# Expert loop written out in program order on three engines, router called for tiles 0-3 and 4-7 behind the next tile's norm

## The chip, the cores and the metric

One core of a Trainium2 chip runs the whole kernel. The metric is device time in microseconds (us), the median of three runs.

## What is computed

Two blocks after each other on a sequence of 1024 tokens of width 1024, in fp32. The first block has two layers, each a mixer, a layer norm, a mixture of experts and a layer norm. The change touches the mixture of experts and what stands around it. The second block (two layers of retention, latent attention and gated linear attention) is not touched.

```python
# hier_moe, cut: 1024 tokens, 4 groups of 8 experts, two experts for each token
gate = g_p * softmax(top_v)                 # of the two best experts in the best group
expert_id = g_idx[:, None] * 8 + top_i
...
def run_block(args):                        # one block of up to 128 tokens of one expert
    xb, e = args
    h = silu(xb @ w_gate[e]) * (xb @ w_up[e])
    return h @ w_down[e]                    # w_gate, w_up 1024 x 512; w_down 512 x 1024
...
out = zeros((N, D)).at[tok_pad].add(y * w_pad[:, None])
# layer: h = layer_norm(ALPHA * h + mix); h = layer_norm(ALPHA * h + hier_moe(h))
```

## The kernel before

**Products.** A product in fp32 is made of three passes with rounded operands (`mm3`, lines 85 to 87): high by high, high by low, low by high. So each operand is first cut by `split` (lines 80 and 81): ScalarE copies the rounded high part, VectorE subtracts it to get the low part. Below, "hi" is the L80 copy and "lo" the L81 subtraction. `lo_eng` can send the subtraction to GpSimd.

**One expert.** Its tokens are gathered into `xg` by an indirect DMA that GpSimd issues (L718), turned by TensorE (L95), and cut into `xgh` and `xgl`. The weights come as six pieces of 1 MB: gate and up for the first half of the inner size, gate and up for the second half, and two of down. They are called g0, u0, g1, u1, d0 and d1 below. Each piece is loaded into one of nine raw slots by SyncE's queue, and cut into one of four `wcut` buffers. The products gate and up end in `gu` (two accumulators in PSUM), then come silu (L743, ScalarE) and the product of both (L744, VectorE), the turn of the result (L754) with its cut into `hh` and `hl`, the down product into the two `accy`, and its scaling in two halves `yo` (L772 on ScalarE, L773 on VectorE). GpSimd issues the scatter of `yo` (L774). The loop runs over 32 experts. In it the down product of expert e-1 stands behind gate and up of expert e, and the gather of expert e+3 behind that; there are four `xg` buffers.

**What sets the order.** A scheduler orders the instructions of each engine. It starts from the order in which the code issues them, and moves an instruction ahead of others where its own estimate has it ready. An engine then runs its instructions strictly in the order that results. Nothing in the code of before ties the loop to an order.

**Ahead of the loop.** `proj_ln` projects the mixer's output for eight tiles of 128 tokens, adds the residual (L923) in two halves n = 0 and 1, and normalizes (lines 468 to 477). For tile t-1 it then turns the normalized rows (`turn`, L568) and multiplies them with the router's weights (`logits`, L578), between the products of tile t; tile 7 has its own call at the end. `logits` adds the bias on VectorE (L579) and calls `route` at the end of tiles 3, 5 and 7, for the tiles (0,4), (4,6) and (6,8). `route` is a chain of some 35 small VectorE instructions. In it M (L633) lets TensorE make the positions `pos` (L636), those make the match matrix A (L691), and TensorE sums A with the codes in `Bm` to the slot table `tb` and the gates `tg` (L704). After the last call the table becomes the index `idx` (L708), on which the first gather waits.

Expert 0's four weight pieces are cut while `proj_ln` still runs, and their lo parts go to GpSimd (the argument `None if e else nc.gpsimd`).

Of the kernel before, what the change touches and what calls it, by code (L numbers as in the profile page):

```python
# [19 lines left out]
S = 1024  # L20
# [49 lines left out]
class Ctx:  # L70
# [18 lines left out]
    def transpose_split(self, src, hi, lo, ps):  # L89

        nc = self.nc
        for g in range(2):
            tp = ps.tile([P, 4, P], F32, tag="tp", name=self.name("tp"))
            for k in range(4):
                nc.tensor.transpose(tp[:, k], src[4 * g + k], self.ident)  # L95
            self.split(tp, hi[:, 4 * g:4 * g + 4], lo[:, 4 * g:4 * g + 4])
# [366 lines left out]
def layer_norm(g, pool, z, dst, gb, eps=1e-5):  # L463
# [11 lines left out]
    for c in range(2):  # L475
        sl = slice(c * 512, c * 512 + 512)
        nc.vector.scalar_tensor_tensor(dst[:, sl], z[:, sl], rs, gb[:, 1, sl], op0=ALU.mult, op1=ALU.add)
# [34 lines left out]
class Moe:  # L512
# [12 lines left out]
    def __init__(self, g, layer, wp, pool, h, hd, yd):  # L525
# [11 lines left out]
        self.views, self.raws = [], []  # L537
# [35 lines left out]
    def logits(self, t, hT, ps):  # L573
# [31 lines left out]
    def route(self, t0, t1, pool, ps):  # L605
# [38 lines left out]
        if t1 == NT:  # L644
            self.slots()
# [35 lines left out]
    def windows(self, pool, t0, t1):  # L681
# [9 lines left out]
        B.tensor_tensor(A, g.iota[:, None, None, :].broadcast_to(shape), self.pos[:, :, ts, None].broadcast_to(shape), op=ALU.is_equal)  # L691
# [14 lines left out]
    def slots(self):  # L706

        self.g.nc.vector.tensor_scalar(self.idx, self.tb, 2.0 * S, None, op0=ALU.add)  # L708
# [11 lines left out]

    def x_t(self, xg, pool, ps):
        g = self.g
        xh = pool.tile([P, KD, P], F32R, tag="xgh", name=g.name("xgh"))
        xl = pool.tile([P, KD, P], F32R, tag="xgl", name=g.name("xgl"))
        g.transpose_split(pair_blocks(xg), xh, xl, ps)
        return xh, xl

    def gate_up(self, wg, wu, x, pool, ps, lo_eng=None, between=None):
        g, nc = self.g, self.g.nc
        acc = [ps.tile([P, 512], F32, tag=f"acc{j}", name=g.name("gu")) for j in range(2)]  # L730
        for kb in range(2):
            if kb == 1 and between is not None:
                between()
            for j, w in enumerate((wg, wu)):
                if w is None:
                    wh, wl = self.next_w(lo_eng)
                else:
                    wh, wl = self.one_w(self.rows(w, kb))
                for k in range(4):
                    kk = 4 * kb + k  # L740
                    g.mm3(acc[j], x[0][:, kk], x[1][:, kk], wh[:, k], wl[:, k], kk == 0, kk == KD - 1)
# [16 lines left out]
    def down(self, wd, mid, xg, gate, yidx, pool, ps, no_dep):  # L758

        g, nc = self.g, self.g.nc  # L760
        hh, hl = mid
        y = pool.tile([P, D], F32, tag="yo", name=g.name("yo"))
        cols = [slice(n * 512, n * 512 + 512) for n in range(2)]
        accs = [ps.tile([P, 512], F32, tag="accy", name=g.name("accy"), bufs=2) for _ in cols]
        for kb in range(2):
            wh, wl = self.next_w() if wd is None else self.one_w(self.down_rows(wd, kb))
            for acc, sl in zip(accs, cols):
                for j in range(2):
                    k = 2 * kb + j
                    g.mm3(acc, hh[:, k], hl[:, k], wh[:, j, sl], wl[:, j, sl], k == 0, k == 3)  # L770
        for acc, sl in zip(accs, cols):
# [9 lines left out]
    def run(self, xgs, ahead):  # L781
# [4 lines left out]
        with tc.tile_pool(name=g.name("moe"), bufs=2, **near) as pool, tc.tile_pool(name=g.name("moeps"), bufs=2, space=PSUM, **near) as ps:  # L786
# [4 lines left out]
            down = lambda e, mid: self.down(None, mid, buf(e), self.sg[:, :, e:e + 1], self.idx[:, 1, e:e + 1], pool, ps, no_dep)  # L791
# [1265 lines left out]
```

## Time and profile before

| | |
|---|---|
| median of 3 runs | 3633.43 us (3632.14 to 3643.11) |
| the profiled execution | 3632.52 us, of which span 3630.7 us |
| mean granted clock of TensorE | 0.952 |
| TensorE busy | 3325.3 us (92%) |
| VectorE busy | 2443.4 us (67%) |
| ScalarE busy | 1818.7 us (50%) |
| GpSimd busy | 821.1 us (23%) |

The span runs from the first to the last instruction on the chip; the profiled execution takes 1.8 us more than that. In the rows below PE is TensorE, PEld its weight load, DVE VectorE, ACT ScalarE, POOL GpSimd and SP SyncE. A busy share is an average over stages that have different limits. The mixtures of experts lie at 721 to 1316 us (first layer) and 1637 to 2232 us (second layer).

### The profile page before, as it was taken

How to read it: one execution, taken by the hardware profiler on the slowest of the kernel's cores; microseconds unless marked ns; L12 is line 12 of the kernel's file. 1: busy time of each engine (PE TensorE's matmuls, PEld its weight loads, DVE VectorE, ACT ScalarE, POOL GpSimd, SP SyncE). 2: the span in 40 equal slices, each digit the busy share in tenths (PEclk: the TensorE clock that was granted, in tenths of full speed). 3: DMA queues.
4: the chain of work that ended last, by engine and by line, in shares of the span. 5: the costliest groups of instructions: out<-in, count | busy, mean ns of one | idle time of the engine just before them, and what ended most of it. 6: DMA issues, size and time to landing. Idle time of an engine off the chain costs nothing.

```text
span 3630.7 us, 44256 instructions
## 1 busy us (share of the span) xinstructions
PE 3325.3 (92%) x16820; PEld 2733.2 (75%) x16820; DVE 2443.4 (67%) x2912; ACT 1818.7 (50%) x2509; POOL 821.1 (23%) x591
## 2 busy tenths in 40 slices
PE   8889899799999969979999995799989899998988
PEld 7777787688887758768888774686777688776876
DVE  5564887699999976568999998634256435324753
ACT  3113673288877743317887774222457411234761
POOL 0000441333321123032332222424002113300120
PEclk9999999799999989989999997899999999998999
DMA  6554623499999960248999996211222542122245
GB/s 224 183 205 145 160 70 138 159 345 387 377 354 359 346 242 24 95 141 316 382 388 362 358 350 248 79 38 24 84 94 83 179 130 40 29 69 97 75 125 161
DMA packets 289358, 695.79 MB, mean 192 GB/s; under 512 B 43898, under 2 KB 140956, under 8 KB 272692
## 3 DMA queue, kind: packets, MB, share of 16 engines
q1 hardware_dynamic: 268404, 650.91, 51.7%
q0 software_dynamic: 18432, 33.60, 2.5%
q10 hardware_dynamic: 2304, 8.39, 0.6%
q8 instruction: 135, 2.21, 0.2%
q14 instruction: 83, 0.68, 0.1%
HBM read 625.59 MB, written 98.66 MB: 199 GB/s over the span
## 4 chain that ended last, share of the span: by engine, by line
PE 46%; DVE 7%; ACT 3%; issue 3%; POOL 3%; DMA 2%; SPq 0%; POOLq 0%; ACTq 0%; DVEq 0%
PE A L87 4%; PE A L85 4%; PE A L86 4%; PE acc L87 3%; PE acc L85 3%; PE acc L86 3%; PE gu L86 3%; PE gu L87 2%; PE gu L85 2%; DVE wcut L81 2%; PE accy L85 1%; PE accy L87 1%; PE accy L86 1%; PE T L1717 1%; PE o L1738 1%
## 5 line engine op out<-in xcount | busy, mean ns | idle before, releaser
L81 DVE TENSOR_TENSOR wcut<-wraw,wcut 128x2048 fp32r<-128x2048 f32 (+1 forms) x393 | 879.7, 2266 | 74.0 <-ACT wcut L80 70.9
L80 ACT ACTIVATE wcut<-wraw 128x2048 fp32r<-128x2048 f32 (+1 forms) x401 | 752.8, 1898 | 90.9 <-PE gu L87 47.1
L86 PE MATMUL gu<-wcut,xgh 128*128 128x512 f32 x1024 | 412.6, 403 | 14.0 <-DVE wcut L81 13.9
L85 PE MATMUL gu<-wcut,xgh 128*128 128x512 f32 x1024 | 404.7, 399 | 0.0
L87 PE MATMUL gu<-wcut,xgl 128*128 128x512 f32 x1024 | 402.8, 393 | 0.0
L774 POOL DMA_INDIRECT yd<-yo,idx x64 | 187.2, 2925 | 857.5 <-DVE yo L773 836.2
L85 PE MATMUL A<-h,whi 128*128 128x512 f32 (+1 forms) x736 | 286.6, 390 | 6.2 <-ACT h L80 3.3
L87 PE MATMUL A<-h,wlo 128*128 128x512 f32 (+1 forms) x736 | 281.3, 382 | 3.8 <-DVE wlo L81 3.8
L86 PE MATMUL A<-h,whi 128*128 128x512 f32 (+1 forms) x736 | 282.2, 384 | 0.9 <-DVE h L81 0.9
L86 PEld LDWEIGHTS gu<-wcut,xgh 128*128 128x128 f32 x1024 | 193.8, 189 | 74.6 <-DVE wcut L81 37.6
L80 ACT ACTIVATE whi<-wraw 128x1024 fp32r<-128x1024 f32 (+2 forms) x86 | 71.1, 856 | 333.8 <-PE A L86 249.8
L87 PEld LDWEIGHTS gu<-wcut,xgl 128*128 128x128 f32 x1024 | 193.1, 189 | 38.1 <-DVE xgl L81 0.5
L85 PEld LDWEIGHTS gu<-wcut,xgh 128*128 128x128 f32 x1024 | 192.0, 189 | 39.1 <-ACT xgh L80 0.5
L86 PE MATMUL accy<-wcut,hh 128*128 128x512 f32 x512 | 203.1, 397 | 0.0
L81 DVE TENSOR_TENSOR wlo<-wraw,whi 128x1024 fp32r<-128x1024 f32 (+2 forms) x86 | 82.5, 975 | 178.1 <-ACT whi L80 177.8
L87 PE MATMUL accy<-wcut,hl 128*128 128x512 f32 x512 | 200.6, 392 | 1.1 <-DVE hl L81 1.1
L85 PE MATMUL accy<-wcut,hh 128*128 128x512 f32 x512 | 191.7, 393 | 0.0
L85 PEld LDWEIGHTS A<-h,whi 128*128 128x128 f32 x736 | 144.4, 197 | 34.3 <-ACT h L80 4.5
L87 PEld LDWEIGHTS A<-h,wlo 128*128 128x128 f32 x736 | 143.7, 195 | 31.4 <-DVE wlo L81 4.7
L86 PEld LDWEIGHTS A<-h,whi 128*128 128x128 f32 x736 | 144.3, 196 | 27.3 <-issue 3.1
L718 POOL DMA_INDIRECT xg<-hd,idx x64 | 136.4, 2131 | 44.9 <-DVE idx L708 24.1
L772 ACT ACTIVATE yo<-accy,sg 128x512 f32<-128x512 f32 x128 | 87.2, 681 | 105.2 <-PE accy L87 105.2
(509 smaller groups left out, 7847.9 us busy)
## 6 DMA issues: line engine op xcount, KB each, us to landing
wraw<-in_moe_w_gate SPq DMA_DIRECT2D x128, 1024.0 KB
wraw<-in_moe_w_up SPq DMA_DIRECT2D x128, 1024.0 KB
wraw<-in_moe_w_down SPq DMA_DIRECT2D x128, 1024.0 KB
spare<-in_ada_w SPq DMA_DIRECT2D x48, 512.0 KB
wraw<-in_w_in SPq DMA_DIRECT2D x40, 512.0 KB
y<-yd SPq DMA_DIRECT2D x16, 1024.0 KB
wraw<-in_attn_w_qkv SPq DMA_DIRECT2D x12, 1024.0 KB
mx<-mixd SPq DMA_DIRECT2D x24, 512.0 KB
```

Of the source, the lines that this page charges most:

```text
L80: self.nc.scalar.activation(hi, src, AF.Copy)
L81: (lo_eng or self.nc.vector).tensor_tensor(lo, src, hi.bitcast(F32), op=ALU.subtract)
L85: mm(out, wh, xh, start=start, stop=False)
L86: mm(out, wh, xl, start=False, stop=False)
L87: mm(out, wl, xh, start=False, stop=stop)
L718: self.g.nc.gpsimd.indirect_dma_start(out=xg, out_offset=None, in_=self.hd, in_offset=bass.IndirectOffsetOnAxis(ap=idx, axis=0), bounds_ch ...
L772: nc.scalar.activation(y[:, sl], acc, AF.Copy, scale=gate[:, 0])
L774: st = nc.gpsimd.indirect_dma_start(out=self.yd, out_offset=bass.IndirectOffsetOnAxis(ap=yidx, axis=0), in_=y, in_offset=None, bounds_chec ...
L1717: nc.tensor.transpose(tp[:, j - j0], p[:, j * P:j * P + P], g.ident)
L1738: nc.tensor.matmul(o, vv[j // 4][:, j % 4, h], pT[:, j], start=j == 0, stop=j == i)
```

## The change

**The loop.** It is written out over 34 steps. Step e issues the result of expert e-2, the gather of expert e+2, gate and up of expert e, the turn of the middle of expert e-1, the turns of the tokens of expert e+1, and the down product of expert e-1. The cuts stand between them, three pieces ahead of TensorE. `in_order` chains every instruction of TensorE, ScalarE and VectorE in the loop to the one that was issued before it on the same engine, so that the scheduler leaves them in program order; it adds no wait. GpSimd and the DMA queues are not chained. The first four gathers are issued ahead of the loop (before: three).

**The router.** `logits` returns its accumulator, and the bias and `route` become `routed`, which is called behind the layer norm of the next tile with `issue_after(normed)`: the scheduler may issue them only after the last instruction of that norm. `route` is called for the tiles (0,4) and (4,8).

**Expert 0's cuts.** All lo parts are now on VectorE. The third piece is issued behind A of the last `route` (`matched`) and the fourth behind `idx` (`slots`).

```diff
+    @contextmanager
+    def in_order(self, *engines):
+        traced = self.nc.cur_bb.bb.instructions
+        n, last = len(traced), {}
+        yield
+        for i in reversed(traced[:n]):
+            last.setdefault(i.engine, i)
+        for i in traced[n:]:
+            if i.engine in engines:
+                if i.engine in last:
+                    self.tc.add_manual_dep(i, last[i.engine].name, mybir.DependencyInfo(mybir.DependencyClass.NoSync, ...
+                last[i.engine] = i
...
-    def next_w(self, lo_eng=None):
-        if not self.raws:
+    def cut(self):
+        if not self.raws and self.views:
             self.prefetch(1)
-        return self.wp.split(self.raws.pop(0), lo_eng)
+        if self.raws:
+            after = self.after.pop(0) if self.after else None
+            with ExitStack() if after is None else self.g.tc.issue_after(after):
+                self.cuts.append(self.wp.split(self.raws.pop(0)))
...
-        nc.vector.tensor_add(self.lg[:, t], lp[:, :36], self.br)
-        for t0, t1 in ((0, 4), (4, 6), (6, 8)):
+        return t, lp
+
+    def routed(self, t, lp, ps):
+        self.g.nc.vector.tensor_add(self.lg[:, t], lp[:, :36], self.br)
+        for t0, t1 in ((0, 4), (4, 8)):
             if t + 1 == t1:
                 self.route(t0, t1, self.rt, ps)
...
         if t1 == NT:
-            self.slots()
+            matched = self.matched.ins
+            self.after = [None, None, matched, self.slots()]
...
-            for e in range(3):
+            for e in range(4):
                 gather(e)
-            nxt = self.x_t(buf(0), pool, ps)
-            for e in range(32):
...
-                nsg = self.gate_up(None, None, x, pool, ps, None if e else nc.gpsimd, between)
-                if e > 0:
-                    down(e - 1, mid[0])
-                if e + 3 < 32:
-                    gather(e + 3)
-                sg = nsg
-            down(31, self.turn_mid(sg, pool, ps))
+            x = self.x_t(buf(0), pool, ps)
+            for _ in range(3):
+                self.cut()
+            with g.in_order(mybir.EngineType.PE, mybir.EngineType.Activation, mybir.EngineType.DVE):
+                for e in range(34):
+                    self.cut()
+                    if e > 1:
+                        result(e - 2, acc)
+                        if e + 2 < 32:
+                            gather(e + 2)
...
+                    if gu:
+                        self.gu(gu[0], x, self.cuts.pop(0), 0)
+                        self.cut()
+                        self.gu(gu[1], x, self.cuts.pop(0), 0)
+                    if 0 < e < 33:
+                        mid = self.turn_mid(sg, pool, ps)
+                    if e + 1 < 32:
+                        nxt = self.x_new(pool)
+                        self.x_half(buf(e + 1), nxt, 0, ps)
+                    if gu:
+                        self.cut()
+                        self.gu(gu[0], x, self.cuts.pop(0), 1)
+                        if e + 1 < 32:
+                            self.x_half(buf(e + 1), nxt, 1, ps)
...
+                        nc.scalar.activation(sg, gu[0], AF.Silu)
+                        self.cut()
+                        self.gu(gu[1], x, self.cuts.pop(0), 1)
+                        nc.vector.tensor_mul(sg, sg, gu[1])
+                        x = nxt
+                    if 0 < e < 33:
...
+                        for kb in range(2):
+                            if gu:
+                                self.cut()
+                            self.dn(acc, mid, self.cuts.pop(0), kb)
...
-                        moe.logits(t - 1, hT, ps)
+                        done = moe.logits(t - 1, hT, ps)
                 zn = z[:, n * 512:n * 512 + 512]
                 nc.vector.scalar_tensor_tensor(zn, zn, ALPHA, acc[n], op0=ALU.mult, op1=ALU.add)
-            layer_norm(g, pool, z, z, gb)
+            normed = layer_norm(g, pool, z, z, gb)
+            if done is not None:
+                with tc.issue_after(normed):
+                    moe.routed(*done, ps)
...
-        moe.logits(NT - 1, moe.turn(NT - 1, ps, pool), ps)
+        moe.routed(*moe.logits(NT - 1, moe.turn(NT - 1, ps, pool), ps), ps)
```

What stands in a row is shown at three places. The line numbers of the changed kernel are others: `route`'s M is L659 there, A is L719, `idx` L736, the residual L980, the norm 485 to 494, the router's bias L605, silu L855, `yo` L804 and L805.

VectorE, first layer, around the residual of tile 7 (`h_5427`, half n = 1 on `acc_6402`), before; the rows ahead of the residual are the end of the route of tiles 4 and 5:

```order
L698 TENSOR_TENSOR Bm_6360<-OH_6040,gt_6043 128x2x32
L641 TENSOR_TENSOR pm_6357<-OH_6040,pos_6350 128x128
L698 TENSOR_TENSOR Bm_6360<-OH_6040,gt_6043 128x2x32
L642 TENSOR_REDUCE posk_6042<-pm_6357 128x2x2
L691 TENSOR_TENSOR A_6363<-iota,posk_6042 128x512
L923 SCALAR_TENSOR_TENSOR h_5427<-h_5427,acc_6402 128x512
L579 TENSOR_TENSOR lg_5441<-lp_6466,br_5438 128x36
L468 BN_STATS st_6477<-h_5427 128x6
```

And in the changed kernel, around the same residual (`acc_6332`):

```order
L81 TENSOR_TENSOR wcut_6585<-wraw_5445,wcut_6585 128x2048
L980 SCALAR_TENSOR_TENSOR h_5427<-h_5427,acc_6331 128x512
L485 BN_STATS st_6406<-h_5427 128x6
L81 TENSOR_TENSOR wcut_6588<-wraw_5447,wcut_6588 128x2048
L980 SCALAR_TENSOR_TENSOR h_5427<-h_5427,acc_6332 128x512
L485 BN_STATS st_6406<-h_5427 128x6
L487 BN_AGGR mv_6409<-st_6406 128x2
L489 TENSOR_SCALAR v_6411<-mv_6409 128x1
```

The route of tiles 4 and 5 has left this place, and two lo parts of expert 0's weights have come to it.

VectorE, first layer, between A of the last route and the index, before:

```order
L691 TENSOR_TENSOR A_6560<-iota,posk_6042 128x512
L669 TENSOR_REDUCE mc_6597<-cnt_6588 128x1
L671 TENSOR_SCALAR rr_6599<-rounds,mc_6597 128x8
L673 TENSOR_REDUCE rn_6601<-rr_6599 128x1
L675 CAST nround_6603<-rn_6601 128x1
L708 TENSOR_SCALAR idx_6044<-tb_6046 128x64
```

And in the changed kernel:

```order
L719 TENSOR_TENSOR A_6490<-iota,posk_6055 128x1024
L699 TENSOR_SCALAR rr_6537<-rounds,mc_6535 128x8
L81 TENSOR_TENSOR wcut_6591<-wraw_5449,wcut_6591 128x2048
L736 TENSOR_SCALAR idx_6057<-tb_6059 128x64
L741 COPY sg_6058<-tb_6060 128x32
```

A covers four tiles instead of two, and one lo part stands between it and the index.

ScalarE, first layer, one expert from silu to silu, before (a late expert; the early ones have both `yo` rows next to each other):

```order
L743 ACTIVATE sgu_10009<-gu_9914 128x512
L80 ACTIVATE wcut_10034<-wraw_10032 128x2048
L80 ACTIVATE wcut_10063<-wraw_10061 128x2048
L772 ACTIVATE yo_10012<-accy_10013,sg_6045 128x512
L80 ACTIVATE wcut_10080<-wraw_10078 128x2048
L772 ACTIVATE yo_10012<-accy_10014,sg_6045 128x512
L80 ACTIVATE hh_10095<-tp_10097 128x512
L80 ACTIVATE xgh_10104<-tp_10106 128x512
L80 ACTIVATE wcut_10122<-wraw_10120 128x2048
L80 ACTIVATE wcut_10139<-wraw_10137 128x2048
L80 ACTIVATE xgh_10104<-tp_10113 128x512
L80 ACTIVATE wcut_10162<-wraw_10160 128x2048
```

And in the changed kernel, for every expert in the middle of the loop:

```order
L855 ACTIVATE sgu_8060<-gu_7987 128x512
L80 ACTIVATE wcut_8064<-wraw_8062 128x2048
L80 ACTIVATE wcut_8084<-wraw_8082 128x2048
L80 ACTIVATE wcut_8101<-wraw_8099 128x2048
L80 ACTIVATE wcut_8118<-wraw_8116 128x2048
L804 ACTIVATE yo_8121<-accy_8080,sg_6058 128x512
L804 ACTIVATE yo_8121<-accy_8081,sg_6058 128x512
L80 ACTIVATE wcut_8148<-wraw_8146 128x2048
L80 ACTIVATE hh_8163<-tp_8165 128x512
L80 ACTIVATE xgh_8172<-tp_8174 128x512
L80 ACTIVATE wcut_8183<-wraw_8181 128x2048
L80 ACTIVATE xgh_8172<-tp_8198 128x512
```

Both `yo` rows have moved behind four cuts (g0, u0 and g1 of the next expert, then its u1), where before they stood behind the second and the third.

## Rows read from the trace of the kernel before

**Rows 1.** Busy time by stretch; each stretch begins and ends at a silu.
```profile
744.21:959.25 215.04, 215.04 (x1009) 179.56 (x1008) 205.54 (x145) 175.24 (x145) 83.99 (x24) 1.00 1.00 382
1030.91:1277.99 247.08, 241.19 (x1098) 193.26 (x1097) 224.10 (x158) 185.68 (x157) 47.66 (x25) 1.00 0.93 346
1659.84:1874.94 215.10, 215.10 (x1009) 179.56 (x1008) 205.57 (x145) 175.25 (x145) 84.05 (x24) 1.00 1.00 379
1946.61:2193.75 247.14, 241.23 (x1098) 193.26 (x1097) 224.10 (x158) 185.71 (x157) 48.08 (x25) 1.00 0.93 344
```

**Rows 2.** ScalarE's timeline, an early expert: start, duration, engine, line, [idle before <-releaser].
```profile
877.43 0.67 ACT L772 ACTIVATE yo<-accy,sg 128x512 f32<-128x512 f32 x1
878.36 0.69 ACT L772 ACTIVATE yo<-accy,sg 128x512 f32<-128x512 f32 x1 [0.25 <-PE accy L87]
```

**Rows 3.** ScalarE's timeline, a late expert.
```profile
1126.44 3.71 ACT L80 ACTIVATE wcut<-wraw 128x2048 fp32r<-128x2048 f32 x2
1133.17 0.69 ACT L772 ACTIVATE yo<-accy,sg 128x512 f32<-128x512 f32 x1 [3.02 <-PE accy L87]
```

**Rows 4.** Waits of PEld, 1031 to 1278 us: total us, times, longest.
```profile
PEld gu L86 <- DVE wcut L81: 16.8, 26, 0.8
```

**Rows 5.** VectorE's timeline, an early expert.
```profile
875.47 4.49 DVE L81 TENSOR_TENSOR wcut<-wraw,wcut 128x2048 fp32r<-128x2048 f32 x2
888.02 0.68 DVE L81 TENSOR_TENSOR hl<-tp,hh 128x512 fp32r<-128x512 f32 x1
```

**Rows 6.** GpSimd's timeline, an early expert.
```profile
863.64 5.01 POOL L774 DMA_INDIRECT yd<-yo,idx  x1 [10.50 <-DVE yo L773]
868.95 2.12 POOL L718 DMA_INDIRECT xg<-hd,idx  x1 [0.30 <-issue]
```

**Rows 7.** Tile xg, 800 to 950 us: from issue to landing, 8 gathers.
```profile
DMA to landing us min/median/max: 8.8/9.2/9.7
```

**Rows 8.** TensorE's timeline, first layer, tile 7.
```profile
671.66 0.39 PE L86 MATMUL acc<-wcut,ah 128*128 128x512 f32 x1
...
674.19 0.39 PE L85 MATMUL acc<-wcut,ah 128*128 128x512 f32 x1
677.75 0.21 PE L636 MATMUL pos<-M,tri_b 128*128 128x64 bf16 x1 [3.18 <-DVE M L633]
...
683.89 3.62 PE L704 MATMUL tb<-Bm,A 128*128 128x64 f32 x16 [2.09 <-DVE A L691]
```

**Rows 9.** VectorE's timeline, first layer, tile 7.
```profile
679.06 4.77 DVE L691 TENSOR_TENSOR A<-iota,posk 128x512 f32<-128x512 f32 x1
688.99 0.69 DVE L923 SCALAR_TENSOR_TENSOR h<-h,acc 128x512 f32<-128x512 f32 x1 [5.15 <-PE acc L87]
692.25 0.20 DVE L579 TENSOR_TENSOR lg<-lp,br 128x36 f32<-128x36 f32 x1 [2.57 <-PE lp L578]
...
695.10 5.64 DVE L477 SCALAR_TENSOR_TENSOR h<-h,rs_y,gb 128x512 f32<-128x512 f32 x2 [0.44 <-POOL rs_y L120]
...
711.72 0.69 DVE L691 TENSOR_TENSOR A<-iota,posk 128x512 f32<-128x512 f32 x1
...
714.47 0.22 DVE L708 TENSOR_SCALAR idx<-tb 128x64 int32<-128x64 f32 x1 [1.31 <-PE tb L704]
```

**Rows 10.** GpSimd's timeline, first layer, tile 7.
```profile
678.74 9.47 POOL L81 TENSOR_TENSOR wcut<-wraw,wcut 128x2048 fp32r<-128x2048 f32 x2 [4.13 <-ACT wcut L80]
```

**Rows 11.** TensorE's timeline, second layer, tiles 6 and 7.
```profile
1578.03 1.12 PE L568 MATMUL tp<-ident,h 128*128 128x128 f32 x4 [4.19 <-DVE h L477]
...
1593.73 0.48 PE L85 MATMUL acc<-wcut,ah 128*128 128x512 f32 x1
```

**Rows 12.** VectorE's timeline, second layer, tiles 6 and 7.
```profile
1612.84 1.42 DVE L477 SCALAR_TENSOR_TENSOR h<-h,rs_y,gb 128x512 f32<-128x512 f32 x2 [0.44 <-POOL rs_y L120]
...
1619.66 3.04 DVE L598 TENSOR_TENSOR goh<-lg,gmx 128x8 f32<-128x8 f32 x1
...
1630.83 0.22 DVE L708 TENSOR_SCALAR idx<-tb 128x64 int32<-128x64 f32 x1 [1.31 <-PE tb L704]
```

More of the change, by code (lines that the diff above doesn't have):

```diff
@@ L1 @@
 import math
-from contextlib import ExitStack
+from contextlib import ExitStack, contextmanager
 import numpy as np
@@ L89, in transpose_split, with turn_half @@
     def transpose_split(self, src, hi, lo, ps):
-        nc = self.nc
         for g in range(2):
[L93 to L96, printed above, removed]
+            self.turn_half(src[4 * g:4 * g + 4], hi[:, 4 * g:4 * g + 4], lo[:, 4 * g:4 * g + 4], ps)
+    def turn_half(self, src, hi, lo, ps):
+        tp = ps.tile([P, 4, P], F32, tag="tp", name=self.name("tp"))
+        for k in range(4):
+            self.nc.tensor.transpose(tp[:, k], src[k], self.ident)
+        self.split(tp, hi, lo)
+    @contextmanager
[8 more added lines that the diff above has]
+                if i.engine in last:
+                    self.tc.add_manual_dep(i, last[i.engine].name, mybir.DependencyInfo(mybir.DependencyClass.NoSync, mybir.DependencyReason.DATA), reason="in_order")
+                last[i.engine] = i
     def load_raw(self, view, pool, tag, b=None):
@@ L476, in layer_norm @@
         sl = slice(c * 512, c * 512 + 512)
-        nc.vector.scalar_tensor_tensor(dst[:, sl], z[:, sl], rs, gb[:, 1, sl], op0=ALU.mult, op1=ALU.add)
+        last = nc.vector.scalar_tensor_tensor(dst[:, sl], z[:, sl], rs, gb[:, 1, sl], op0=ALU.mult, op1=ALU.add)
+    return last.ins
 def norm_stats(g, pool, z, eps=1e-5):
@@ L536, in __init__ @@
         wg, wu, wd = (a[n][layer] for n in ("moe_w_gate", "moe_w_up", "moe_w_down"))
-        self.views, self.raws = [], []
+        self.views, self.raws, self.cuts = [], [], []
         for e in range(33):
@@ L706, in slots @@
     def slots(self):
-        self.g.nc.vector.tensor_scalar(self.idx, self.tb, 2.0 * S, None, op0=ALU.add)
+        return self.g.nc.vector.tensor_scalar(self.idx, self.tb, 2.0 * S, None, op0=ALU.add).ins
     def slot_gates(self):
@@ L719, in gather, with x_new, x_half, gu @@
             in_offset=bass.IndirectOffsetOnAxis(ap=idx, axis=0), bounds_check=S - 1, oob_is_err=False)
+    def x_new(self, pool):
+        return [pool.tile([P, KD, P], F32R, tag=tag, name=self.g.name(tag)) for tag in ("xgh", "xgl")]
+    def x_half(self, xg, x, q, ps):
+        self.g.turn_half(pair_blocks(xg)[4 * q:4 * q + 4], *(y[:, 4 * q:4 * q + 4] for y in x), ps)
     def x_t(self, xg, pool, ps):
[L722 to L728, printed above, removed]
+        x = self.x_new(pool)
+        for q in range(2):
+            self.x_half(xg, x, q, ps)
+        return x
+    def gu(self, acc, x, w, kb):
+        for k in range(4):
+            kk = 4 * kb + k
+            self.g.mm3(acc, x[0][:, kk], x[1][:, kk], w[0][:, k], w[1][:, k], kk == 0, kk == KD - 1)
+    def gate_up(self, wg, wu, x, pool, ps):
         g, nc = self.g, self.g.nc
@@ L731, in gate_up @@
         for kb in range(2):
-            if kb == 1 and between is not None:
-                between()
             for j, w in enumerate((wg, wu)):
[L735 to L741, printed above, removed]
+                self.gu(acc[j], x, self.one_w(self.rows(w, kb)), kb)
         sg = pool.tile([P, 512], F32, tag="sgu", name=g.name("sgu"))
@@ L756, in turn_mid, with dn, result @@
         return hh, hl
-    def down(self, wd, mid, xg, gate, yidx, pool, ps, no_dep):
+    def dn(self, accs, mid, w, kb):
+        for n, acc in enumerate(accs):
+            for j in range(2):
+                k = 2 * kb + j
+                sl = slice(n * 512, n * 512 + 512)
+                self.g.mm3(acc, mid[0][:, k], mid[1][:, k], w[0][:, j, sl], w[1][:, j, sl], k == 0, k == 3)
+    def result(self, accs, xg, gate, yidx, pool, no_dep):
         g, nc = self.g, self.g.nc
-        hh, hl = mid
         y = pool.tile([P, D], F32, tag="yo", name=g.name("yo"))
[L763 to L771, printed above, removed]
+        for n, acc in enumerate(accs):
+            sl = slice(n * 512, n * 512 + 512)
             nc.scalar.activation(y[:, sl], acc, AF.Copy, scale=gate[:, 0])
@@ L835, in run @@
                     sg = self.gate_up(one(wg), one(wu), x, pool, ps)
-                    self.down(one(wd), self.turn_mid(sg, pool, ps), xg, gc, ic[:, 1], pool, ps, None)
+                    acc = [ps.tile([P, 512], F32, tag="accy", name=g.name("accy"), bufs=2) for _ in range(2)]
+                    mid = self.turn_mid(sg, pool, ps)
+                    for kb in range(2):
+                        self.dn(acc, mid, self.one_w(self.down_rows(one(wd), kb)), kb)
+                    self.result(acc, xg, gc, ic[:, 1], pool, None)
     def combine(self, t, y, z, pool):
@@ L902, in mm @@
                 g.mm3(acc, a[0][:, k], a[1][:, k], wh[:, k % 4], wl[:, k % 4], k == order[0], k == order[-1])
-        a = cut(0)
+        a, done = cut(0), None
         for t in range(NT):
```

14 lines of the change are left out of this document (6 added, 8 removed).

## The prediction

> **What bounds the kernel now.** I read the table of engines first, then busy time by stretch over the two expert loops, the waits and ScalarE's timeline in a fast and a slow stretch, and last the timelines of the stretch that leads into each loop.
>
> The stretches begin and end at a silu, so they give the period of one expert. For 12 experts of the first layer it is 215.04 / 12 = 17.92 us, with TensorE busy all the time; the next 13 of the steady stretch take 247.08 / 13 = 19.01 us each, with TensorE idle for 5.9 us in all. The second layer shows the same two periods [rows 1]. In the fast stretch TensorE is the bound and VectorE is close behind: 205.54 / 12 = 17.13 us of 17.92. In the slow one no engine is full. What differs there is an order: ScalarE waits 3.02 us at the first `yo` for the down product, and the two `yo` no longer stand together [rows 3], as they do in the fast stretch, where the wait is 0.25 us [rows 2]. A cut stands behind that wait and its lo behind the cut, and so TensorE's weight loads wait for VectorE's lo, 26 times, 16.8 us together [rows 4]. So the slow period comes from the order that the scheduler chose, not from work.
>
> The second place is the end of `proj_ln`. With tile 7 TensorE waits for M of tiles 4 and 5 (3.18 us) and for A (2.09 us) [rows 8]. Beside GpSimd's lo parts [rows 10], VectorE's A of the same shape takes 4.77 us instead of 0.69, and the last two steps of the norm 5.64 us [rows 9] instead of 1.42 [rows 12]. This is the chain on which the first gather waits, so all of it counts.
>
> **Part 1: the loop in program order.** The work of an expert stays: 72 products, 12 turns, six cuts. I laid one period of the new order out by hand, from 0 at g0, with a cut at 1.9 us, a lo at 2.2 us (two in 4.49 [rows 5]) and 0.7 us for hl and the like. `yo` ends on VectorE at 5.9; the lo of d0 at 8.0, of d1 at 11.4 (TensorE wants them at 12.3 and 15.1); the lo of the next g0 at 15.1 (wanted at 17.9), u0 at 17.9 (wanted at 21.1), g1 at 20.1 (wanted at 24.3). TensorE never waits, so I take 17.92 us, the measured period of an order much like it, for all experts. Then the slow stretches fall away: 247.08 - 13 x 17.92 = 14.1 us in the first layer, the same in the second: **-28.2 us**. The experts between the stretches add up to 17.92 each, within 0.1 us, and give nothing. From below, the period can't get shorter than TensorE's own work: with the products 0.23 us apart [rows 8] and turns at 0.11 it is 17.9. From above, VectorE has 0.79 us of slack and is now bound to an order; that is the first rival.
>
> At the loop's end the middle of expert 31 is turned and cut with nothing of TensorE's beside it: four turns (0.6 us with their tail), the hi (0.6) and hl (0.68 [rows 5]), 2 us a layer: **+4 us**.
>
> The gathers come one step later than before: expert e+2 in step e, behind the scatter of e-2, as both use one `xg` buffer. GpSimd takes 5.01 us for the scatter [rows 6], so the gather is issued at 5.9 + 0.3 + 5.0 + 0.3 = 11.5 and lands 9.2 us later (8.8 to 9.7 [rows 7]), at 20.7. TensorE turns those rows at 6.0 of the next period, 23.9. 3.2 us of cover: I cost it at nothing; without that cover each us late costs about 60 us, 30 times in each layer.
>
> **Part 2: tile 7, first layer.** The products of half n = 1 are 24; the twelfth starts at 674.19, and they are 0.23 us apart until M stops them [rows 8]. Without the route of tiles 4 and 5 among them they end at 674.19 + 12 x 0.23 + 0.4 = 677.4, where the residual starts; it starts at 688.99 now [rows 9]. From there to the index it now takes 714.47 - 688.99 = 25.5 us. Of this the stretched norm goes, 5.64 - 1.42 = 4.2, and the wait of 2.57 for the router's product, behind which the norm's statistics stand [rows 9]; the bias is issued behind the norm now. That leaves 18.7. The route of four tiles instead of two adds 1.3 (an estimate: A of twice the size 0.6 more at most by its 0.69, the other 35 rows 0.02 each), and eight more of the sums stand before the index: half of the 16 in 3.62 us [rows 8], 1.8. So 21.8, the index at 699.2: **-15.3 us**.
>
> **Part 3: tile 7, second layer.** The half n = 1 starts at 1593.73 and, without the wait of 4.19 for the stretched norm of tile 6 [rows 11], at 1589.5; 24 products later, at 1595.4, comes the residual, and after the same 21.8 the index: 1617.2 instead of 1630.83 [rows 12], **-13.6 us**. Part of it is a comparison of eight columns that took 3.04 us [rows 12].
>
> **Part 4: what comes in its place.** Four lo parts a layer come back to VectorE, 2.2 us each. The first two stand at tile 7's residuals, under TensorE's 5.5 us of products; the third stands between A and the index, under 3.6 us of sums; the fourth behind the index, under the gather. I cost them at nothing; without that cover they are 8 x 2.2 = 17.6 us, the high end of this term. The positions of tiles 0 to 3 now wait for a norm of the next tile, and TensorE's products are queued behind them: no row of before shows this wait. Its bounds are 0 and the 3.18 that M costs now [rows 8], in each layer; I take 1.5 us for both together, since the norm beside it is no longer stretched.
>
> **Sum.** -28.2 + 4 - 15.3 - 13.6 + 1.5 = -51.6 us. The profiled execution took 3632.5 us (0.9 under the median of 3633.4), so 3581 us. With TensorE's period at 17.8, the positions free and the end's turn half hidden it is 3581 - 62 x 0.1 - 1.5 - 2 = 3571; with all lo parts on the chain and 3.18 for each M wait 3581 + 17.6 + 4.9 = 3603.
>
> **A rule against this change.** The transfers move 382 GB/s in the fast stretch with their engines busy throughout, 346 in the slow one [rows 1]. The Trainium skill, "DMA: Bandwidth & Descriptors", under "Specifications" and "Where 436 GB/s comes from", gives about 358 GB/s as the limit of one core's transfers between HBM and SBUF. By that rule no order could hold 17.92: the period would be 17.92 x 382 / 358 = 19.1 us, and the sum would come out at some 3652. The trace disagrees, with 382 held for 215 us in one layer and 379 in the other.
>
> **Rivals.**
> 1. *The program order makes a wait that the free order avoids, and every expert takes the slow period.* Place: VectorE, whose next lo stands behind hl, xgl or `yo` until TensorE or ScalarE has finished theirs; its slack is 0.79 us [rows 1]. For it: in the slow stretch exactly such a wait spreads from ScalarE to TensorE. Against: the new order keeps both `yo` together, like the fast one. Price: the 17 experts that are fast now take 1.09 us more, 18.5 us a layer, and the 28.2 stay: 3632.5 - 28.9 + 5.5 + 37 = 3646 us, slower. It decides from a period of 17.92 + 51.6 / 62 = 18.75 us.
> 2. *The gather lands after TensorE wants it.* For it: one step less than before, and a scatter of 5 us ahead. Against: 3.2 us of cover. At 2 us too late 3581 + 120 = 3701 us.
> 3. *The transfers bound the period at 19.1*: 62 x 1.18 = 73 more than my sum, 3581 + 73 = 3654 us; by the 382 GB/s of rows 1 unlikely.
> 4. *Only one half comes.* The loop gains but the lo parts and M waits eat the heads: 3632.5 - 28.2 + 4 = 3608. Or the heads gain and the order leaves a slow stretch as long as now: 3632.5 - 28.9 + 1.5 = 3605.
>
> **How the numbers follow.** The forecast of 3581, between 3569 and 3598, has a chance of 0.74; rival 4 has 0.13; rival 1 0.07; rivals 2 and 3 0.03 each. The range of 3567 to 3609 holds the first two. Under 0.3%, about 11 us, a measurement of this kernel can't tell a difference: faster means under 3622, slower over 3644. Faster gets 0.85 (the first two less a little for a rival 4 worse than its price), same 0.05 (that, and a period near 18.75), slower 0.10.
>
> **What would show it.** Right: all silu 17.92 us apart in both layers, no PE or PEld wait between them, the index of the first layer near 699 and of the second 15.3 + 14.1 - 2 + 13.6 = 41 us earlier than now, no stretched A or norm, lo parts on VectorE only. Wrong: silu 18.5 us apart or more (then the wait that comes before TensorE's names the step); a wait of TensorE's turn for `xg`; a lo part between the norm's rows; a long wait for M at tile 4 or 5.

## The result and the profile after

The changed kernel takes 3571.7 us (median of 4 runs, 3567.0 to 3576.1) against 3634.3 of before: a ratio of 0.9827, 95% interval 0.9816 to 0.9839. That is 62.6 us less; the forecast was 51.6 less, 3581, with a range of 3567 to 3609. The profiled execution is the slowest of the four, 3576.1 us with a span of 3574.3.

Busy time by stretch, from the second silu to the last but one, 29 experts in each layer. The columns are those of [rows 1]: the stretch and its length, busy time and instructions of PE, PEld, DVE, ACT and POOL, the granted clock of TensorE, the busy share of the DMA engines, and GB/s.

```profile
730.50:1249.99 519.49, 519.49 (x2438) 433.89 (x2437) 496.62 (x349) 417.04 (x350) 168.70 (x57) 1.00 0.99 375
1614.46:2133.95 519.49, 519.49 (x2437) 433.89 (x2436) 496.63 (x349) 417.04 (x349) 168.71 (x57) 1.00 0.99 375
```

519.49 / 29 = 17.91 us for every expert of both layers, with TensorE busy without a gap. The slow stretches of [rows 1] are gone. The transfers hold 375 GB/s over all of it.

VectorE's timeline at tile 7 of the first layer, the answer to [rows 9], and the index of the second layer, the answer to [rows 12]:

```profile
677.03 0.69 DVE L980 SCALAR_TENSOR_TENSOR h<-h,acc 128x512 f32<-128x512 f32 x1 [0.68 <-PE acc L87]
...
680.51 1.41 DVE L494 SCALAR_TENSOR_TENSOR h<-h,rs_y,gb 128x512 f32<-128x512 f32 x2 [0.44 <-POOL rs_y L137]
681.84 0.19 DVE L605 TENSOR_TENSOR lg<-lp,br 128x36 f32<-128x36 f32 x1
...
693.82 1.22 DVE L719 TENSOR_TENSOR A<-iota,posk 128x1024 f32<-128x1024 f32 x1
694.96 0.23 DVE L699 TENSOR_SCALAR rr<-rounds,mc 128x8 f32<-128x8 f32 x1
695.09 2.29 DVE L81 TENSOR_TENSOR wcut<-wraw,wcut 128x2048 fp32r<-128x2048 f32 x1
698.80 0.23 DVE L736 TENSOR_SCALAR idx<-tb 128x64 int32<-128x64 f32 x1 [1.43 <-PE tb L732]
...
1582.90 0.23 DVE L736 TENSOR_SCALAR idx<-tb 128x64 int32<-128x64 f32 x1 [1.44 <-PE tb L732]
```

The first index comes at 698.8 (forecast 699.2; 714.5 before), the second at 1582.9, 47.9 us earlier than before (forecast 41). None of the rows shown is stretched, and the lo part behind A ends at 697.4, before the sums that the index waits for.

TensorE's timeline in the same place, the answer to [rows 8]:

```profile
656.99 0.22 PE L662 MATMUL pos<-M,tri_b 128*128 128x128 bf16 x1
...
681.40 1.79 PE L590 MATMUL tp<-ident,h 128*128 128x128 f32 x8 [2.70 <-DVE h L494]
...
691.94 0.27 PE L662 MATMUL pos<-M,tri_b 128*128 128x128 bf16 x1 [5.48 <-DVE M L659]
```

The positions of tiles 0 to 3 (656.99) wait for nothing. What is left are the waits that the chain to the first gather has by itself: the norm, the route and, behind them, the gather.

GpSimd's timeline, one expert of the loop, the answer to [rows 6]:

```profile
869.49 2.81 POOL L806 DMA_INDIRECT yd<-yo,idx  x1 [11.68 <-DVE yo L805]
872.61 3.12 POOL L746 DMA_INDIRECT xg<-hd,idx  x1 [0.30 <-issue]
```

The scatter takes 2.8 us and no longer the 5.0 of the early experts of before; the late ones of before took 1.0. The gather issued at 872.6 is read by TensorE at 887.3; gathers land 9.4 us after their issue here, so there are 5.3 us of cover.

### The profile page after: what moved, and what is told of

Same layout as the page of the kernel before. It is cut to its first block, busy times and chain, and to the rows that moved or that the text cites. A ratio compares the mean times of both kernels' runs of the same rounds, so it can differ in the third digit from the quotient of the medians.

```text
span 3574.3 us, 44065 instructions
## 1 busy us (share of the span) xinstructions
PE 3308.5 (93%) x16808; PEld 2738.9 (77%) x16808; DVE 2424.9 (68%) x2850; ACT 1818.0 (51%) x2505; POOL 817.6 (23%) x583
## 5 line engine op out<-in xcount | busy, mean ns | idle before, releaser
L81 DVE TENSOR_TENSOR wcut<-wraw,wcut 128x2048 fp32r<-128x2048 f32 (+1 forms) x401 | 902.6, 2268 | 74.9 <-ACT wcut L80 74.8
L806 POOL DMA_INDIRECT yd<-yo,idx x64 | 173.5, 2711 | 794.5 <-DVE yo L805 788.0
L746 POOL DMA_INDIRECT xg<-hd,idx x64 | 184.8, 2888 | 56.6 <-DVE idx L736 37.7
L1703 POOL TENSOR_TENSOR z<-z,lo 128x1024 f32<-128x1024 f32 x8 | 19.0, 2376 | 476.6 <-DVE r L81 177.4
```

Of the source, the lines that this page charges most:

```text
L81: (lo_eng or self.nc.vector).tensor_tensor(lo, src, hi.bitcast(F32), op=ALU.subtract)
L746: self.g.nc.gpsimd.indirect_dma_start(out=xg, out_offset=None, in_=self.hd, in_offset=bass.IndirectOffsetOnAxis(ap=idx, axis=0), bounds_ch ...
L806: st = nc.gpsimd.indirect_dma_start(out=self.yd, out_offset=bass.IndirectOffsetOnAxis(ap=yidx, axis=0), in_=y, in_offset=None, bounds_chec ...
```

## Experiments

All medians stand beside 3633 to 3635 us of the kernel before in the same session.

**The two halves apart.** `loop_only` has the new loop, with the router as before and GpSimd's lo parts:

```diff
-        for t0, t1 in ((0, 4), (4, 8)):
+        for t0, t1 in ((0, 4), (4, 6), (6, 8)):
...
-                        done = moe.logits(t - 1, hT, ps)
+                        moe.routed(*moe.logits(t - 1, hT, ps), ps)
```

> Only the written-out loop with its chain; the router (tiles 0-3, 4-5, 6-7, inside the logits) and GpSimd's lo parts for expert 0 stay as before. Theory, that the change is a sum of two independent gains: silu 17.91 us apart in both layers, each loop 14 us shorter and the first layer's last scatter some 3 us earlier, so 31 us less than before, about 3603. TensorE's waits of 3.2 us for M and of 4 to 8 us for the norm of tile 7 stay. Rival, that the loop's gain needs the other half (an index or weights that come earlier): silu over 18.5 us apart again, 3620 or more.

Measured: 3601.7 us, ratio 0.9910 (0.9897 to 0.9924). The silu are 17.91 us apart in both layers, but for the first and the last step, and TensorE's waits ahead of the first loop are those of before:

```profile
PE tp L589 <- DVE h L494: 8.0, 1, 8.0
PE pos L661 <- DVE M L658: 8.0, 2, 4.8
```

`head_only` has the kernel before with the router's new calls and all lo parts on VectorE.

> Only the router's part and expert 0's lo parts on VectorE; the loop's code and its free order stay as before. Theory of two independent gains: the first index at 699 instead of 714, the second layer's some 29 us earlier in all, the late experts still 19.01 us apart, so 29 to 31 us less than before, about 3604. Rival, that the four lo parts on VectorE or the later positions cost what the route gives: within 10 us of before.

Measured: 3605.3 us, ratio 0.9918 (0.9904 to 0.9931). Its busy time in the slow stretch (1014 to 1261 us) is that of [rows 1]:

```profile
1014.00:1261.00 247.00, 241.20 (x1098) 193.26 (x1098) 224.11 (x158) 185.75 (x158) 47.65 (x25) 1.00 0.94 345
```

So the loop gives 32.1 us and the head 28.6, together 60.7 of the 62.6: two gains that add up.

**GpSimd's lo parts alone.** `pool_lo` is the changed kernel with expert 0's lo parts on GpSimd again; its third and fourth piece are no longer held behind A and the index.

```diff
-            after = self.after.pop(0) if self.after else None
-            with ExitStack() if after is None else self.g.tc.issue_after(after):
-                self.cuts.append(self.wp.split(self.raws.pop(0)))
+            self.ncut += 1
+            self.cuts.append(self.wp.split(self.raws.pop(0), self.g.nc.gpsimd if self.ncut <= 4 else None))
```

> The changed kernel with expert 0's four lo parts on GpSimd again. Theory, that part of the gain ahead of the loop is VectorE's rows no longer stretched beside GpSimd's lo parts: stretched rows come back (4 to 10 us instead of 0.7 to 1.4) in the norms or the route of tiles 6 and 7, 5 to 15 us in all over the changed kernel, 3577 to 3587. Rival, that all of it was the route of tiles 4 and 5 that stood among TensorE's products: 3572, no change.

Measured: 3591.1 us, ratio 0.9884 (0.9869 to 0.9900), 19.4 over the changed kernel. GpSimd's and then VectorE's timeline, and TensorE's wait:

```profile
669.20 14.62 POOL L81 TENSOR_TENSOR wcut<-wraw,wcut 128x2048 fp32r<-128x2048 f32 x3 [4.82 <-ACT wcut L80]
683.78 0.54 POOL L137 TENSOR_TENSOR rs_y<-v,mhalf 128x1 f32<-128x1 f32 x1
684.29 4.49 POOL L81 TENSOR_TENSOR wcut<-wraw,wcut 128x2048 fp32r<-128x2048 f32 x1
```

```profile
684.35 5.64 DVE L494 SCALAR_TENSOR_TENSOR h<-h,rs_y,gb 128x512 f32<-128x512 f32 x2 [4.89 <-POOL rs_y L137]
```

```profile
PE tp L589 <- DVE h L494: 11.5, 1, 11.5
```

The cost has two parts, and only one was expected. The norm's last rows are stretched beside a lo part, 5.64 us instead of 1.41. And three lo parts stand ahead of the norm's `rs_y` in GpSimd's queue, so that VectorE waits 4.89 us for a row of half a microsecond. The index comes at 707.3 instead of 698.8. So with these lo parts on GpSimd the new calls keep only about a third of the head's gain.

**The chain.** `no_chain` is the changed kernel with `in_order` replaced by an empty context.

> The changed kernel without the chain: the same code order, but the scheduler may reorder. Theory, that the place of the yo copies between the cuts sets the period: in the order that the scheduler makes now a cut stands between both yo copies in all experts but a few, so the slow period of 19.0 us comes back in most experts of both layers, 20 to 60 us over the changed kernel, 3592 to 3632. Rival, that the new program order by itself is enough: 17.9 us and 3572.

Measured: 3600.7 us, ratio 0.9913 (0.9897 to 0.9930), 29.0 over the changed kernel. Busy time from the fourth silu to the sixteenth and from the nineteenth to the thirty-first:

```profile
764.39:979.44 215.05, 215.05 (x1009) 179.57 (x1008) 205.09 (x147) 175.19 (x144) 62.46 (x25) 1.00 1.00 384
1034.40:1259.76 225.36, 221.61 (x1007) 178.25 (x1006) 205.74 (x145) 171.07 (x145) 51.97 (x23) 1.00 0.94 348
```

Without the chain the late experts take 225.36 / 12 = 18.78 us: the code's order is not enough, the chain is needed. But the early ones run at 17.92 us, though ScalarE's order there has a cut between both `yo`. That contradicts the cause that was expected, and the next four runs look for the right one.

**What makes the slow period.** `yo_apart` moves both `yo` forward in the chained loop: the first now stands ahead of the cuts of g1 and u1, and g1's cut lies between the two.

```diff
-                        result(e - 2, acc)
...
                         for kb in range(2):
-                            if gu:
+                            if gu and kb == 0:
                                 self.cut()
                             self.dn(acc, mid, self.cuts.pop(0), kb)
+                        if e < 32:
+                            result(e - 1, acc, self.cut)
```

> The changed kernel with one cut (g1 of the next expert) moved behind the first yo copy, so that ScalarE's order is silu, cut, cut, yo, cut, yo as in the slow experts of before; the rest of the chain stays. Theory, that this place makes the slow period: the cut and its lo wait for the down product; laid out by hand VectorE stands still for about 0.9 us more than its 0.8 us of slack allows, so 18.0 to 18.4 us for each expert, and up to 19.0 if it is the whole cause; 6 to 65 us over the changed kernel. Rival, that the slow period has another cause (the transfers, the free order of TensorE): 17.91 us and no change.

Measured: 3585.0 us, ratio 0.9859 (0.9844 to 0.9874); silu 18.20 us apart. 13.3 us over the changed kernel and far from 19.0. The wait behind these 0.29 us is another than in the slow experts: TensorE's weight loads wait for `hl` and not for a weight piece (800 to 1200 us).

```profile
PEld tp L98 <- DVE hl L81: 9.7, 22, 0.4
```

`turn_early` moves the turns of the middle and of the next tokens to the start of a step; `slow_order` has both edits.

```diff
...
+                    if 0 < e < 33:
+                        mid = self.turn_mid(sg, pool, ps)
+                    if e + 1 < 32:
+                        nxt = self.x_new(pool)
+                        self.x_half(buf(e + 1), nxt, 0, ps)
+                    self.cut()
                     if gu:
                         self.gu(gu[0], x, self.cuts.pop(0), 0)
                         self.cut()
                         self.gu(gu[1], x, self.cuts.pop(0), 0)
-                    if 0 < e < 33:
-                        mid = self.turn_mid(sg, pool, ps)
...
```

> The changed kernel with the turn of the middle and the first turn of the next tokens at the start of a step instead of behind its first 24 products, and the second turn behind these 24, which is where the slow experts of before have them; ScalarE's order becomes silu, three cuts, yo, yo, hh, xgh, two cuts, xgh, cut. Theory A, that the place of the yo copies makes 0.29 us of the slow period (18.20 with yo apart) and the rest comes with these turns: VectorE's hl and xgl and ScalarE's copies stand ahead of the cuts of u1 and d0, so 18.4 to 18.9 us here. Theory B, the turns don't matter alone: 17.9 to 18.0. Besides, the gathers are wanted 6 us earlier, with a cover of some 5.3 - 6 = -0.7 us: up to 0.35 us for each expert, in a wait for xg that the trace shows apart.

> Both: yo apart and the turns early, which gives ScalarE the order that the slow experts of before have, silu, cut, cut, yo, cut, yo, hh, xgh, cut, cut, xgh, cut, in all experts. Theory, that this order is the whole cause of the slow period: 19.0 us in all experts (and up to 0.35 more in waits for xg), 1.1 x 60 = 66 us over the changed kernel, some 3638, no faster than before. Rival, that something beside the order makes it (the free order's other rows, the transfers): under 18.6 us.

Measured: 3585.8 us (0.9867, 0.9850 to 0.9883) and 3583.8 us (0.9870, 0.9853 to 0.9886). Both have their silu 17.91 us apart; the time over the changed kernel lies mostly in the first step, where the second expert's tokens are wanted at once (17.5 to 18.1 us from the first silu to the second instead of 11.7). So both theories that ScalarE's order makes the slow period fell: in `slow_order` it has, kind for kind, the order of the slow experts, waits 2.20 us for the down product at the first `yo`, and the period does not suffer. The row, and behind it the same one of the next run, `less_lead`:

```profile
1136.23 0.69 ACT L806 ACTIVATE yo<-accy,sg 128x512 f32<-128x512 f32 x1 [2.20 <-PE accy L87]
```

```profile
1134.63 0.69 ACT L806 ACTIVATE yo<-accy,sg 128x512 f32<-128x512 f32 x1 [2.67 <-PE accy L87]
```

`less_lead` differs from `slow_order` in one number: two pieces are cut ahead of the loop instead of three.

```diff
-            for _ in range(3):
+            for _ in range(2):
                 self.cut()
```

> The kernel with yo apart and the turns early, which ran at 17.91 us, with two pieces cut ahead of the loop instead of three, so that every cut is one piece later against the products; piece by piece ScalarE's order is now that of the slow experts of before: silu, cut d1 of the expert before, cut g0 of the next, yo, cut u0, yo, hh, xgh, g1, u1, xgh, d0, silu. Theory, that the slow period comes from how far the cuts are ahead of TensorE and not from the place of yo or the turns: u0's lo ends after TensorE has done g0, and weight loads wait for VectorE's lo some 0.8 us, twice for each expert; 19.0 us, 1.1 x 60 = 66 us over its kernel's 3584, some 3650. Rival, that the lead is long enough and the free order's other rows or the transfers make the period: under 18.3 us, below 3610.

Measured: 3641.3 us, ratio 1.0016 (1.0007 to 1.0025), 57 us over `slow_order`. Busy time over 24 experts of `slow_order`, then of `less_lead`, and the weight loads' wait of `less_lead` from 1031 to 1278 us, which answers to [rows 4]:

```profile
771.10:1201.02 429.92, 429.92 (x2017) 359.10 (x2016) 408.52 (x290) 345.10 (x289) 88.87 (x48) 1.00 1.00 381
```

```profile
772.95:1220.94 447.99, 437.69 (x2017) 359.29 (x2016) 412.69 (x289) 342.37 (x289) 88.85 (x48) 1.00 0.98 366
```

```profile
PEld gu L86 <- DVE wcut L81: 10.5, 14, 0.8
```

429.92 / 24 = 17.91 against 447.99 / 24 = 18.67. So what decides between these two is how many pieces the cuts are ahead of TensorE. When ScalarE comes to the first `yo`, g0 and u0 of the next expert are cut in `slow_order`, and u0's lo is ready in time. In `less_lead`, as in the slow experts of before, only g0 is; u0's cut stands behind the wait for the down product, and its lo ends up to 0.8 us after TensorE wants it.

The same count, taken from the traces at the first `yo` of each expert in the steady loop, answers for the other kernels. In the kernel before the cuts are three pieces past the down product that `yo` reads for experts 0 to 13, two for 14 and 15, and one from 16 on, in both layers, and the period changes at about the same place. In `no_chain` the count is the same, which fits its early experts being fast in spite of the cut between both `yo`. The changed kernel has four all along, `turn_early` three, `yo_apart` and `slow_order` two, `less_lead` one.

The lost piece is 0.76 of the 1.10 us. `less_lead` waits once for each expert, where the kernel before waited twice (26 times in 13 experts [rows 4]); the remaining 0.34 us, with the second wait, lies in the finer order of VectorE or TensorE, which no run took apart.

**VectorE's slack.** `dve_pad1` and `dve_pad2` add one and two products of 128x512 on VectorE for each expert.

```diff
+                        for _ in range(1):     # dve_pad2: 2
+                            nc.vector.tensor_tensor(pad, pad, pad, op=ALU.mult)
```

> The changed kernel with one VectorE product of 128x512 more for each expert, 0.6 us from start to start, behind the product of silu and up. Theory, VectorE has 0.8 us of slack in a period: no change, 17.91 us, within 3 us of the changed kernel. Rival, the fixed order has used the slack up: 0.6 x 62 = 37 us more.

> The same with two such products, 1.2 us. Theory, slack of 0.8 us: the period grows by 0.4 us to 18.3, 25 us over the changed kernel. Rival, slack used up: 1.2 x 62 = 74 us. Rival, more slack than that since waits of VectorE for cuts give way: no change.

Measured: 3577.4 us (0.9845, 0.9832 to 0.9859) with silu 17.99 us apart, and 3625.2 us (0.9977, 0.9967 to 0.9987) with 18.71. VectorE's timeline of `dve_pad2`, and TensorE's wait from 800 to 1200 us:

```profile
902.72 2.29 DVE L81 TENSOR_TENSOR wcut<-wraw,wcut 128x2048 fp32r<-128x2048 f32 x1 [0.37 <-ACT wcut L80]
904.93 0.68 DVE L860 TENSOR_TENSOR sgu<-sgu,gu 128x512 f32<-128x512 f32 x1
905.53 1.41 DVE L862 TENSOR_TENSOR pad<-pad 128x512 f32<-128x512 f32 x2
906.86 6.69 DVE L81 TENSOR_TENSOR wcut<-wraw,wcut 128x2048 fp32r<-128x2048 f32 x3
```

```profile
PE tp L98 <- DVE hl L81: 11.3, 22, 0.5
```

The product of `dve_pad1` takes 0.60 us from start to start and costs 0.07, so 0.53 us of VectorE's slack were free. Two take 1.33 us (905.53 to 906.86) and cost 0.80, again 1.33 - 0.53. VectorE keeps 0.37 us of idle time even then, in the wait for a cut that waits for TensorE, and TensorE waits for hl, whose turn shares its buffer in PSUM with the next one. VectorE is the next bound, half a microsecond behind TensorE.

**The gathers' cover.** `gather_pad` puts 14 fills on GpSimd between scatter and gather, and chains GpSimd too.

```diff
                         if e + 2 < 32:
+                            for _ in range(14):
+                                nc.gpsimd.memset(pad, 0.0)
                             gather(e + 2)
```

> The changed kernel with 14 fills of 128x512 on GpSimd (some 7.5 us) between the scatter and the gather of a step, GpSimd chained too. Theory as in the trace of the changed kernel, where a gather is issued 14.7 us ahead of the turn that reads it and lands in 9.4: cover of 5.3 us, so 2.2 us late for each expert, period about 20.1 us, 2.2 x 58 = 130 us over the changed kernel. By the prediction's cover of 3.2 us: 4.3 us late, 250 us. Rival, that the gathers are far from mattering: no change.

Measured: 3664.6 us, ratio 1.0084 (1.0063 to 1.0106), 93 over the changed kernel. TensorE's turns of three experts after each other:

```profile
901.00 0.72 PE L98 MATMUL tp<-ident,xg 128*128 128x128 f32 x4 [2.71 <-DMA xg<-hd,idx]
...
920.60 0.64 PE L98 MATMUL tp<-ident,xg 128*128 128x128 f32 x4
...
940.99 0.71 PE L98 MATMUL tp<-ident,xg 128*128 128x128 f32 x4 [2.31 <-DMA xg<-hd,idx]
```

The fills take 8.1 us, 2.8 more than the cover of 5.3, and the two waits shown are 2.7 and 2.3 us, near what the trace of the changed kernel gives. But mostly only every second expert waits: in the first loop TensorE waits 16 times for `xg`, 0.5 to 2.9 us, 30.4 in all. A late gather delays TensorE behind the `yo` of its step, so the next gather is issued in time and the next turn, which comes late, finds its rows there. From the first silu to the last that loop takes 45.1 us more than in the changed kernel. The other 14.7 are busy time of TensorE, 562.0 us for work that took 547.3 there: behind the wait at 901.0 the granted clock was 0.51 from 902.0 to 905.4. The price of a late gather is thus about half of what was written (93 us, where 2.8 us at 60 for each are 168).

**TensorE kept at work.** `warm` adds 60 products for each layer, whose results nobody reads, in the waits ahead of the first gather.

```diff
+        with g.in_order(mybir.EngineType.PE):
+            moe.warm(10)
             moe.routed(*moe.logits(NT - 1, moe.turn(NT - 1, ps, pool), ps), ps)   # in route: warm(22), warm(8)
+            moe.warm(20)
```

> The changed kernel with 60 products more for each layer on TensorE, whose results nobody reads, in the waits between tile 7's last product and the first gather (10 while the norm runs, 22 in the route, 8 ahead of A, 20 while the gather is under way). Theory, that the half clock of this stretch (0.50 from 682 to 706 us in the changed kernel) comes from TensorE's waits and costs on the path: T 0.8, logits 1.6, half of the sums 1.8, the turn 0.9, the first products 1.6, together some 6 us a layer, 12 us, 3560. Rival, that the clock does not hold, or that the added products end after the rows they wait beside: no change, or up to 4 us a layer slower.

Measured: 3583.5 us, ratio 0.9862 (0.9845 to 0.9878), 11.8 over the changed kernel. TensorE's timeline:

```profile
680.79 2.55 PE L606 MATMUL warm<-wcut,ah 128*128 128x512 f32 x10
685.10 1.45 PE L590 MATMUL tp<-ident,h 128*128 128x128 f32 x8 [1.75 <-DVE h L494]
686.47 3.63 PE L600 MATMUL lp<-wr,hT 128*128 128x36 f32 x16
689.90 6.74 PE L606 MATMUL warm<-wcut,ah 128*128 128x512 f32 x22
...
699.25 3.76 PE L741 MATMUL tb<-Bm,A 128*128 128x64 f32 x32 [0.28 <-DVE A L728]
...
703.05 6.43 PE L606 MATMUL warm<-wcut,ah 128*128 128x512 f32 x20
709.32 1.11 PE L98 MATMUL tp<-ident,xg 128*128 128x128 f32 x8
```

The half clock does cost: the sums take 3.76 us here at the higher clock, 7.03 in the changed kernel. But with the 10 products 1.75 us of the first wait stay, and the router's product runs at 3.63 us, half clock. The last 20 took 6.4 us, and the first turn stands behind them at 709.3, 5.4 us later than in the changed kernel. And the added products read one of the `wcut` buffers, so that expert 0's last cut waits for them on ScalarE, with `xgh` behind it:

```profile
709.52 1.91 ACT L80 ACTIVATE wcut<-wraw 128x2048 fp32r<-128x2048 f32 x1 [14.99 <-PE warm L606]
```

TensorE then waits 1.5 us for `xgh` and 1.7 for `xgl`, which the changed kernel does not. In the second layer 0.3 us of the first wait stay, the granted clock is 1.00 from 1570 to 1584 us and the router's product takes 1.98 us. Of the 9.6 us by which the profiled execution is longer, 9.3 are there at the first silu of the first layer; the second layer neither gains nor loses. So this run does not show what filling the waits is worth by itself: the buffer that the products hold and their number are mixed in it, and no other number was tried. Nothing measured here beats the changed kernel.

## Why the prediction was right

- **The loop, -28.2 us**: every period of the steady loop is 17.91 us, and `loop_only` gives 32.1. The forecast's +4 for the two ends was wrong in size: the turn of the last middle does cost about 1 us, but the last step, which has no next tokens to turn, is 16.47 us from silu to silu instead of 18.40. From the first product to the last a loop is 14.1 us shorter in the first layer (590.5 to 576.4) and 13.6 in the second. Besides, the first layer's last scatter is issued 1.8 us after the loop's last product and no longer 4.4; it was counted at nothing.
- **Its cause.** The step "a cut stands behind that wait and its lo behind the cut" was right, "the two `yo` no longer stand together" was not: the same order of `yo` and cuts runs at 17.91 when the cuts are one piece further ahead (`slow_order`, `less_lead`), and in the kernel before the late experts have two pieces of lead less than the early ones. The forecast held because the new order is far enough ahead, which the layout by hand had shown piece by piece.
- **The heads, -15.3 and -13.6**: the first index is 15.7 us earlier. From the end of the first loop to the second index another 18.4 us go, of which 3.7 belong to the first layer's end (TensorE's first turns behind the loop are by so much earlier against the loop), so 14.7. `pool_lo` shows that about 18 of these 30 us hang on GpSimd's lo parts, more than the two stretched norms of the forecast (4.2 us in each layer). In its order the norm's `rs_y` stands behind them, with 4.89 us of wait, which it did not in the first layer of the kernel before (0.44 [rows 9]).
- **The positions, +1.5**: no wait in the first layer, 0.3 us in the second. Putting 1.5 us between the bounds here was about one microsecond too much.
- **What hides the lo parts** was as forecast: each of them stands beside TensorE's products, sums or the gather.
- **Rival 1** (VectorE can't keep up in a fixed order) did not come, but was nearer than its price said: free slack is 0.53 us, not 0.79, since part of VectorE's idle time is a wait for a cut that TensorE releases. **Rival 2** had 5.3 us of cover and not 3.2, since the scatter takes 2.8 us here and the forecast had the 5.0 of an early expert; its price of 60 us for each us was about twice what `gather_pad` shows. **Rival 3** falls with 375 GB/s over 519 us in both layers and TensorE busy all the time. The Trainium skill, "DMA: Bandwidth & Descriptors", under "Specifications", gives about 358 GB/s as the limit of one core; this trace does not agree, and the trace decides.

Put together, the last down product of the first loop comes 29.5 us earlier than before and that of the second 61.3, 9.7 more than the sum of 51.6. About 3.5 of these lie in the loops (27.7 against 28.2 - 4), 3.0 in the heads and the positions (30.4 against 28.9 - 1.5) and 3.7 at the first layer's end, less 0.5 by which the first products stand later behind each index. The profiled execution gives 4.9 of this back in the second block, where no instruction changed; the medians, 62.6 us apart, show nothing of it.

## What to carry to other kernels

When an engine shows two periods in one loop, compare piece by piece how far the feeding engines are ahead, not only in which order they run: one piece of lead was worth 0.75 us in 18 here. A scheduler that orders each engine freely can lose that lead along the loop; writing out the order and chaining the engines keeps it, and the code's order without the chain did not. The lead can be counted in a trace: cuts done, less pieces used, at the same row of each expert. Before work is put on an idle engine, look at what stands behind it in that engine's queue and which other engine's rows get longer beside it.

## What the runs showed of the hardware

- VectorE's norm rows of 128x512 took 1.41 us for two alone (changed kernel) and 5.64 beside one GpSimd subtraction of 128x2048 (`pool_lo`), and 10.03 beside two in the second layer of the kernel before.
- GpSimd's time for the same scatter was 5.01 us in the early experts of the kernel before, 1.01 in the late ones, 2.81 in the changed kernel and 1.01 in `slow_order`; for the gather it was 2.12, 2.70, 3.12 and 2.70. No run takes apart why.
- TensorE's clock was at half (0.50, 1.2 of 2.4 GHz) from 682 us on in the changed kernel, after a wait of 2.70 us behind the router's small product; with ten products put into that wait and 1.75 us of it left, it fell all the same, and with 0.32 us left, in the second layer of `warm`, it did not. It also fell without any wait: in the changed kernel it was 0.55 from 664.6 to 668.4, behind the sums of tiles 0 to 3 (32 products of 128x64 in 3.65 us) and with TensorE busy throughout. In `warm` it was 0.72 in the mean from 703 to 709, over the 20 products behind the last sums, with no wait before them.
